# A hybrid decoder block on one core: six SwiGLU pairs from seven products, and the weight sums moved to pay for them

## The chip, the cores and the metric

The kernel runs on one core of a Trainium2 chip. The metric is the device time of one execution, in microseconds; several executions are timed and their median is given. One more execution is recorded by the hardware profiler, and every duration below comes from that one.

## The reference

The block takes 512 rows of 1024 channels in float32. Two token mixers (a Conformer convolution and an RG-LRU) run side by side and are merged through sigmoid gates and a projection. What the change touches is the channel mixer that follows:

```
h = rmsnorm(x, norm2_g)
x = x + (silu(h @ ffn_w1) * (h @ ffn_w3)) @ ffn_w2      # ffn_w1, ffn_w3: 1024 x 2816; ffn_w2: 2816 x 1024
return rmsnorm(x, norm_f_g)
```

## The kernel before

**Products in three parts.** TensorE multiplies float32r. To keep float32's precision every operand is split into a high part (a cast, on ScalarE) and a low part (a subtraction, on VectorE or GpSimd, L113), and a product is the sum of three: high by high, high by low, low by high. A weight chunk is 128 x 1024 values, 512 KB. It is loaded by SyncE's queue into one of four raw buffers (`raws`), cast and split into one of five `hl` buffers, and used by TensorE in 24 matmuls. `weights(key)` sends out the loads of that chunk and of the next four, in a fixed order of chunks.

**Stages, in order.** The input projections (z) follow a list written out by hand, `ORDER`, with 64 steps; the convolution, the gates and the recurrence run beside them on VectorE and ScalarE. GpSimd makes the low parts of the z weights. Then come the two ways out, `yb` (eight steps, weights `lo`) and `ya` (eight steps, weights `co`), then the mixing product `mx`, then the SwiGLU pairs, then the last product `or`, with `ffn_w2`.

**SwiGLU pairs.** The 22 column blocks of the hidden layer are worked in 11 pairs (k and k + 11). A pair of the plain kind takes four chunks, 96 matmuls of 512 columns. Pairs 2 to 5, listed in `SEVEN`, are made by a Strassen-Winograd form: seven block products for eight. Each product takes one chunk, 24 matmuls of 256 columns (`fr`, L1020). Three of the seven weight chunks are quarters of the weights themselves (b11, b21, b22); four are sums of quarters (t1 to t4), read from DRAM. They are used in the order b11, b21, b22, t2, t1, t3, t4. The activations' sums are made by `f_inputs` just before pair 1.

**Who makes the sums.** Those of the SwiGLU weights are made by GpSimd, in `make_f_sums`, a generator that is stepped once per entry of `ORDER` and per step of yb. Every third step it loads a piece (half a chunk's worth of four quarters) into one of three `wsums` buffers; two steps later GpSimd does four operations on it; five weight chunks later SyncE stores it to DRAM. The last product is of seven products too, for all its eleven pairs of blocks, and the sums of its weights (`ows`, then `ot` in DRAM) are made by VectorE, in `make_sums`: two loads of 512 KB into two of the four raw buffers, four operations, four stores of 256 KB. `out_sums` calls it after SwiGLU pairs: two each after pairs 1, 6, 7, 8 and 9, one each after 3 and 5.

**Operands of the last product.** When a pair is complete, `Sevenfold.pair` makes from it five tiles that stay until the last product; those tiles, the activations and their sums share 63 slots (`long`).

**Order on the engines.** Apart from a few stretches written out by hand, a planner orders each engine's instructions: it walks the program in priority of its order and takes what is ready by its own estimate of time. On the chip each queue is then in order. A load that has to wait for its buffer holds up every load behind it on SyncE's queue.

Of the kernel before, what the change touches and what calls it, by code (L numbers as in the profile page):

```python
# [8 lines left out]
F32 = mybir.dt.float32  # L9
F32R = mybir.dt.float32r  # L10
# [3 lines left out]
P = 128  # L14
T = 512
# [25 lines left out]

SEVEN = (2, 3, 4, 5)
SUMS_AT, SUMS_STEP, SUMS_LAG, STORE_LAG = 4, 3, 2, 5


ROWS = [
# [32 lines left out]
def tile_block(ctx, tc, a, out):  # L81
    nc = tc.nc
# [1 line left out]
    consts = pool("consts", 1)  # L84
    raws = pool("raws", RAW)
    hls = pool("hls", HL)
    wsums = pool("wsums", 3)
    psum = pool("psum", 6, space=bass.MemoryType.PSUM)
    psum2 = pool("psum2", 2, space=bass.MemoryType.PSUM)

# [131 lines left out]

    dram = ctx.enter_context(tc.tile_pool(name="dram", bufs=1, space=bass.MemoryType.DRAM))

    class Quartered:
        def __init__(self, name, w, kh, lo, parts=()):

            self.name, self.w, self.kh = name, w, kh
            self.parts = {n: [None] * kh for n in parts}
            self.sums = {(n, k): dram.tile([P, T], F32, tag=f"{name}{n}_{k}", name=f"{name}{n}_{k}") for n in ("t1", "t2", "t3", "t4") if n not in parts for k in range(kh)}  # L230
            self.at = {}

            def quarter(n, k):
                if n[0] == "t":
                    return self.sums[n, k][:, :]
                i, h = int(n[1]) - 1, int(n[2]) - 1
                return w[:, k + kh * i, h * T : (h + 1) * T]

            def chunk(key, of):
                def load(raw_t):  # L240
                    for i, q in enumerate(of):
                        nc.sync.dma_start(raw_t[:, i * T : (i + 1) * T], quarter(*q))

                for i, q in enumerate(of):
                    self.at[q] = (f"{name}{key}", i)
                wchunk(f"{name}{key}", load, len(of), T, lo=lo)


            for p_ in (("b11", "t1", "b21"), ("t2", "t3", "b22"), ("t4",)):
                p_ = [n for n in p_ if n not in parts]  # L250
                for k in range(kh):
                    if len(p_) % 2 and k % 2 == 0:
                        chunk(f"{p_[-1]}_{k}", [(p_[-1], i) for i in (k, k + 1) if i < kh])
                    if len(p_) > 1:
                        chunk(f"{p_[0]}_{k}", [(n, k) for n in p_[:2]])
# [20 lines left out]
        def make_sums(self, k):  # L276
            q = [raws.tile([P, 1024], F32, tag="raw", name=f"{self.name}ws{k}_{i}") for i in range(2)]
            for i, v in enumerate(q):
                nc.sync.dma_start(v, self.w[:, k + self.kh * i, :])
            (q11, q12), (q21, q22) = ((v[:, :T], v[:, T:]) for v in q)  # L280
            sub(vec, q22, q22, q12)
            sub(vec, q12, q12, q11)
            vec.tensor_tensor(out=q11, in0=q22, in1=q11, op=ALU.add)
            sub(vec, q21, q21, q11)
            for n, v in (("t1", q12), ("t2", q11), ("t3", q22), ("t4", q21)):
                if n in self.parts:
                    self.parts[n][k] = split(f"{self.name}{n}{k}", v, vec)
                else:
                    nc.sync.dma_start(self.sums[n, k][:, :], v)

    mixq = Quartered("mx", a["w_mix_out"][0].rearrange("(k p) n -> p k n", p=P), ND // 2, vec, ("t1", "t4"))
    w1 = a["ffn_w1"][0].rearrange("(k p) n -> p k n", p=P)
# [1 line left out]


    KF = NF // 2
    F_SUMS = ("t2", "t1", "t4", "t3")
    f_sums = {k: dram.tile([P, 4, 1024], F32, tag=f"fs{k}", name=f"fs{k}") for k in SEVEN}

    def f_quarter(n, k, w_, c0, c1):  # L300
# [4 lines left out]
    def f_chunk(n, k):  # L305
        def load(raw_t):
            if n[0] == "t":
                nc.sync.dma_start(raw_t, f_sums[k][:, F_SUMS.index(n), :])
            else:
                for i, w_ in enumerate((w1, w3)):  # L310
                    nc.sync.dma_start(raw_t[:, i * T : (i + 1) * T].rearrange("p (k n) -> p k n", k=4), f_quarter(n, k, w_, 0, 4))

        wchunk(f"f{n}_{k}", load, 8, P, lo=vec)

    def make_f_sums():

        todo = [(k, i, c) for k in SEVEN for i in range(2) for c in (0, 2)]
        sums_due, stores_due = [], []  # L320
        n = 0
        while todo or sums_due or stores_due:
            if stores_due and emitted[0] >= stores_due[0][0]:
                stores_due.pop(0)[1]()
            if sums_due and n >= sums_due[0][0]:
                sums_due.pop(0)[1]()
            if todo and n >= SUMS_AT and (n - SUMS_AT) % SUMS_STEP == 0:
                k, i, c = todo.pop(0)
                raw = wsums.tile([P, 1024], F32, tag="wsum", name=f"fws{k}_{i}_{c}")
                q = [raw[:, 256 * m : 256 * m + 256] for m in range(4)]  # L330
                four = (w1, w3)[i].rearrange("p (h k) (e n) -> p h k e n", h=2, e=2)
                with tc.issue_after(newest["load"]):
                    for h in range(2):
                        nc.sync.dma_start(
                            raw[:, h * T : h * T + T].rearrange("p (e k n) -> p e k n", e=2, k=2),
                            four[:, h, c : c + 2, :, k * P : (k + 1) * P].rearrange("p k e n -> p e k n"),
                        )

                def sums(raw=raw, q=q, k=k, at=T * i + P * c):
                    q11, q12, q21, q22 = q  # L340
                    with tc.issue_after(newest["sub"]):
                        sub(pool_e, q22, q22, q12)
                        sub(pool_e, q12, q12, q11)
                        pool_e.tensor_tensor(out=q11, in0=q22, in1=q11, op=ALU.add)
                        sub(pool_e, q21, q21, q11)

                    def stores():
                        with tc.issue_after(newest["load"]):
                            nc.sync.dma_start(f_sums[k][:, :, at : at + 256], raw.rearrange("p (m n) -> p m n", m=4))

                    stores_due.append((emitted[0] + STORE_LAG, stores))

                sums_due.append((n + SUMS_LAG, sums))
            n += 1
            yield
# [437 lines left out]
            mixq.make_sums(j // 2 - 1)  # L793
    yb = sgb
    run_beside(1000)
    for _ in f_sums_steps:
        pass


    add = lambda o, x, y: vec.tensor_tensor(out=o, in0=x, in1=y, op=ALU.add)  # L800
# [8 lines left out]

    class Sevenfold:  # L810
        def __init__(self, q):
            self.q, self.uv, self.ops = q, [], []
            self.name, self.kh = q.name, q.kh

        def tile(self, j, make):

            k, i = j % self.kh, j // self.kh
            if i == 0:
                self.uv.append((longt(f"{self.name}u{k}"), longt(f"{self.name}v{k}")))
            for dst, cs in zip(self.uv[k], HALVES):  # L820
                make(cs, dst[:, HALVES[i]])
            if i:
                self.pair(k, *self.uv[k])

        def pair(self, k, ua, va):

            n = self.name
            u_ = split(f"{n}us{k}", ua, vec)
            s1 = shortt(f"{n}s1{k}")[:, LO]
            add(s1, va[:, LO], va[:, HI])  # L830
            sp = longt(f"{n}s1p{k}", F32R)
            split_to(sp[:, LO], sp[:, HI], s1, vec)
            e = longt(f"{n}e{k}")
            sub(vec, e[:, HI], ua[:, LO], va[:, LO])
            sub(vec, va[:, LO], s1, ua[:, LO])
            sub(vec, e[:, LO], ua[:, HI], va[:, LO])
            self.ops.append((u_, sp, e, va))
# [58 lines left out]
    for n, j in enumerate(mixq.order()):  # L896
        ws = w_tiles(f"co{j}", ND)
        ps = bank(f"ya{j}")
        mm3(ps, ws, un)
        o = sga[j]  # L900
        vec.scalar_tensor_tensor(out=o, in0=ps, scalar=pc("conv_b_out", j), in1=o, op0=ALU.add, op1=ALU.mult)
        m7.tile(j, lambda cs, dst: add(dst, o[:, cs], yb[j][:, cs]))
        if n == 0:
            mixq.make_sums(3)


    x2 = [[longt(f"x2{t}{h}") for h in range(2)] for t in range(NT)]
# [46 lines left out]


    o7 = Sevenfold(outq)
    sums_of = iter(range(KF))

    def out_sums(n):

# [50 lines left out]
    def ffn_seven(k):  # L1011
# [30 lines left out]
        c12 = shortt(f"c12_{k}")  # L1042
        add(c12, r3, q)
        out_of(c12, u_[:, HI])
        product(r7, "s3", "t3")
        c21 = shortt(f"c21_{k}")
        act.copy(c21, r7)
# [3 lines left out]
        add(c21, r1, c21)  # L1051
        out_of(c21, v_[:, LO])
        o7.uv.append((u_, v_))
        o7.pair(k, u_, v_)

    for k in range(1, KF):
        if k in SEVEN:
            ffn_seven(k)
            out_sums(k % 2)
            continue  # L1060
        for j in (k, k + KF):
            p1, p3 = bank(f"f1_{j}"), bank(f"f3_{j}")
            mm3(p1, w_tiles(f"f1_{j}", ND), h2)
            mm3(p3, w_tiles(f"f3_{j}", ND), h2)
            ffn_out(j, p1, p3)
        out_sums(2 if k < KF - 1 else KF)


    x2 = [[longt(f"x2b{t}{h}") for h in range(2)] for t in range(NT)]
# [93 lines left out]
```

## Time and profile before

| | |
|---|---|
| median of 3 runs | 814.86 us (813.67 to 815.19) |
| profiled execution | 814.89 us, of which its span is 813.0 us |
| granted TensorE clock, mean | 0.995 |
| TensorE matmuls busy | 800.0 us, 98% of the span |
| VectorE busy | 644.1 us, 79% |
| ScalarE busy | 443.1 us, 55% |
| GpSimd busy | 210.3 us, 26% |
| DMA | 153.46 MB, 189 GB/s on average |

The span is the time from the first to the last instruction; the execution's own time also holds what lies around it. Busy times overlap between engines. Matmuls are pipelined, so that the durations of single ones overlap too, and a row of the chain, with its length over its count, tells the rate. All times inside the execution are counted from the start of the span.

### The profile page before, as it was taken

To read this page: it belongs to the slowest core of one execution; us is meant where nothing else is said; L and a number is where in the kernel's file an instruction comes from. 1 tells how busy PE (TensorE), PEld (TensorE's weight loads), DVE (VectorE), ACT (ScalarE), POOL (GpSimd) and SP (SyncE) were. 2 spreads that over 40 slices of the span, in tenths; PEclk is the share of its full clock that TensorE was granted. 3 is DMA by queue.
4 is the path that set the end of the run, shared out by engine and by line. 5 is a ranking of instruction groups with operands and counts; after the bars stand their busy time and mean duration, and the time that the engine had idled before them with its cause. 6 is when DMAs were issued, how large, how long until landed. Compare 5 with 4: busy or idle time off the path is not lost.

```text
span 813.0 us, 11453 instructions
## 1 busy us (share of the span) xinstructions
PE 800.0 (98%) x4038; PEld 683.3 (84%) x4038; DVE 644.1 (79%) x1010; ACT 443.1 (55%) x626; POOL 210.3 (26%) x156
## 2 busy tenths in 40 slices
PE   8999999999999999999999999999999999999996
PEld 7988888888887888888888898999988888888884
DVE  4699899998999987777878769797875664688456
ACT  7546688776687755653336554364632223476442
POOL 3565768766675740000000042000000000000000
PEclk9999999999999999999999999999999999999998
DMA  6646475666654522358638535788778778576542
GB/s 209 193 123 171 136 202 176 189 193 198 186 170 130 182 75 65 116 171 263 217 104 259 156 97 176 238 262 248 224 247 282 249 271 297 177 250 216 169 160 104
DMA packets 182029, 153.46 MB, mean 189 GB/s; under 512 B 12519, under 2 KB 150163, under 8 KB 181971
## 3 DMA queue, kind: packets, MB, share of 16 engines
q1 hardware_dynamic: 181971, 152.72, 60.7%
q8 instruction: 32, 0.52, 0.3%
q14 instruction: 26, 0.21, 0.1%
HBM read 123.46 MB, written 26.21 MB: 184 GB/s over the span
## 4 chain that ended last, share of the span: by engine, by line
PE 93%; DVE 4%; issue 1%; DMA 1%; SPq 0%; POOL 0%; ACT 0%; POOLq 0%
PE z L441 31%; PE f L441 19%; PE or L844 13%; PE fr L1020 10%; PE yb L441 7%; PE ya L441 5%; PE mxr L844 5%; DVE cv L600 2%; PE g L721 2%; DMA raw_in<-in_w_in_dram 1%; PE th L481 0%; DVE xb L745 0%; PE tx L481 0%; DVE of L1086 0%; SPq L397 0%
## 5 line engine op out<-in xcount | busy, mean ns | idle before, releaser
L600 DVE SCALAR_TENSOR_TENSOR cv<-u,par,cv 128x511 f32<-128x511 f32 (+17 forms) x240 | 162.6, 729 | 1.1 <-ACT cv L597 0.9
L113 POOL TENSOR_TENSOR hl_in<-raw_in,hl_in 128x1024 fp32r<-128x1024 f32 x52 | 125.5, 2418 | 94.0 <-ACT hl_in L117 92.0
L117 ACT CAST hl_in<-raw_in 128x1024 fp32r<-128x1024 f32 x52 | 54.3, 1044 | 5.9 <-PE z L441 3.0
L117 ACT CAST hl_f<-raw_f 128x1024 fp32r<-128x1024 f32 x28 | 29.3, 1050 | 49.1 <-DMA raw_f<-in_ffn_w_dram 36.0
L113 DVE TENSOR_TENSOR hl_ob<-raw_ob,hl_ob 128x1024 fp32r<-128x1024 f32 (+1 forms) x23 | 27.1, 1178 | 26.8 <-ACT hl_ob L117 26.6
L113 DVE TENSOR_TENSOR hl_f<-raw_f,hl_f 128x1024 fp32r<-128x1024 f32 x28 | 36.2, 1304 | 14.3 <-ACT hl_f L117 14.2
L994 POOL TENSOR_TENSOR hf<-h20h,h20l 128x512 f32<-128x512 f32 x1 | 1.3, 1287 | 171.8 <-DVE h20l L485 171.8
L117 ACT CAST hl_ob<-raw_ob 128x1024 fp32r<-128x1024 f32 (+1 forms) x23 | 23.4, 1015 | 40.3 <-PE or L844 17.4
L441 PE MATMUL z<-h10h,hl_in 128*128 128x512 f32 (+1 forms) x112 | 42.4, 380 | 2.7 <-DVE h10l L485 1.5
L441 PE MATMUL z<-h15h,hl_in 128*128 128x512 f32 (+1 forms) x112 | 42.0, 376 | 0.0
L441 PE MATMUL z<-h16h,hl_in 128*128 128x512 f32 (+1 forms) x112 | 42.0, 376 | 0.0
L441 PE MATMUL z<-h17h,hl_in 128*128 128x512 f32 (+1 forms) x112 | 41.9, 376 | 0.0
L441 PE MATMUL z<-h11h,hl_in 128*128 128x512 f32 (+1 forms) x112 | 41.8, 375 | 0.0
L441 PE MATMUL z<-h12h,hl_in 128*128 128x512 f32 (+1 forms) x112 | 41.8, 375 | 0.0
L441 PE MATMUL z<-h14h,hl_in 128*128 128x512 f32 (+1 forms) x112 | 41.8, 375 | 0.0
L441 PE MATMUL z<-h13h,hl_in 128*128 128x512 f32 (+1 forms) x112 | 41.8, 375 | 0.0
L113 POOL TENSOR_TENSOR fws<-fws 128x256 f32<-128x256 f32 x48 | 36.3, 756 | 2.3
L113 DVE TENSOR_TENSOR ows<-ows,ows 128x512 f32<-128x512 f32 x22 | 15.2, 689 | 20.6 <-DMA ows<-in_ffn_w_dram 20.4
L113 DVE TENSOR_TENSOR hl_ot<-raw_ot,hl_ot 128x1024 fp32r<-128x1024 f32 (+1 forms) x17 | 20.1, 1191 | 11.1 <-ACT hl_ot L117 10.7
L441 PEld LDWEIGHTS z<-h10h,hl_in 128*128 128x128 f32 x112 | 21.3, 191 | 7.4 <-DVE h10l L485 1.8
L117 ACT CAST hl_ot<-raw_ot 128x1024 fp32r<-128x1024 f32 (+1 forms) x17 | 17.5, 1028 | 16.5 <-PE or L844 14.8
L441 PEld LDWEIGHTS z<-h15h,hl_in 128*128 128x128 f32 x112 | 21.4, 191 | 3.8
(905 smaller groups left out, 2574.9 us busy)
## 6 DMA issues: line engine op xcount, KB each, us to landing
raw_in<-in_w_in_dram SPq DMA_DIRECT2D x52, 512.0 KB
raw_f<-in_ffn_w_dram SPq DMA_DIRECT2D x28, 512.0 KB
ows<-in_ffn_w_dram SPq DMA_DIRECT2D x22, 512.0 KB
ot<-ows SPq DMA_DIRECT2D x44, 256.0 KB
raw_ob<-in_ffn_w_dram SPq DMA_DIRECT2D x33, 256.0 KB
raw_ot<-ot SPq DMA_DIRECT2D x33, 256.0 KB
fws<-in_ffn_w_dram SPq DMA_DIRECT2D x32, 256.0 KB
fs<-fws SPq DMA_DIRECT2D x16, 512.0 KB
```

What stands on the lines that cost most here:

```text
L113: return eng.tensor_tensor(out=o, in0=x, in1=y, op=ALU.subtract)
L117: copy(h, full)
L441: pe.matmul(ps, l, r, start=i == 0, stop=i == n - 1)
L600: vec.scalar_tensor_tensor(out=acc[c][:, s:], in0=u[c][:, : T - s], scalar=dw(c, s), in1=acc[c][:, s:], op0=ALU.mult, op1=ALU.add)
L721: pe.matmul(ps, l, r, start=k == 0, stop=k == len(mms) - 1)
L844: pe.matmul(banks[i], l_[:, ts], r_, start=start and n == 0, stop=stop and n == 2, skip_group_check=again)
L994: pool_e.tensor_tensor(out=v, in0=h2p[c][0].bitcast(F32), in1=h2p[c][1].bitcast(F32), op=ALU.add)
L1020: pe.matmul(ps[:, HALVES[i]], lw[:, 4 * i + c, :], rx_, start=not (again or i or c or m), stop=bool(i and c == 3 and m == 2), skip_group_c ...
```

## The change

`SEVEN` grows from four pairs to six, 2 to 7, so GpSimd has 24 pieces to make for 16. It also makes the sums of the first two of the last product's weights (`OUT_EARLY`), four more pieces of the same size, so 28 in all. From step 55 on a piece is begun every second step, and the generator is stepped through the eight steps of ya as well. The other nine sums of the last weights stay with VectorE; `OUT_SUMS` places them after pairs 1 (three), 2, 4, 6, 7 (one each) and 8 (two). A sum is stored by two transfers of 512 KB, since the four sums of a block now lie side by side in DRAM. A pair's operands for the last product are no longer always made at once: those of seven-product pairs wait and are released inside the next pair (pair 6's not before pair 8). For pairs 0 to 2 one of the operands lies in the three `wsums` buffers.

```diff
-SEVEN = (2, 3, 4, 5)
+PIECES = 3
+OUT_EARLY = 2
+OUT_SUMS = {1: 3, 2: 1, 4: 1, 6: 1, 7: 1, 8: 2}
+SEVEN = (2, 3, 4, 5, 6, 7)
 SUMS_AT, SUMS_STEP, SUMS_LAG, STORE_LAG = 4, 3, 2, 5
+SUMS_DENSE = 55
...
+            if not self.parts:
+                for i, v in enumerate(q):
+                    nc.sync.dma_start(self.all_sums[k][:, 2 * i : 2 * i + 2, :], v.rearrange("p (m n) -> p m n", m=2))
+                return
...
-        todo = [(k, i, c) for k in SEVEN for i in range(2) for c in (0, 2)]
+        todo = [f_piece(k, i, c) for k in SEVEN for i in range(2) for c in (0, 2)]
+        todo += [o_piece(k, c) for k in range(OUT_EARLY) for c in range(2)]
...
-            if todo and n >= SUMS_AT and (n - SUMS_AT) % SUMS_STEP == 0:
+            if todo and n >= next_at:
+                next_at += SUMS_STEP - (n >= SUMS_DENSE)
...
             if i:
-                self.pair(k, *self.uv[k])
+                self.waiting.append((k, *self.uv[k]))
+                self.release()
+
+        def release(self, keep=0):
+
+            while len(self.waiting) > keep:
+                self.pair(*self.waiting.pop(0))
...
-            u_ = split(f"{n}us{k}", ua, vec)
+            p_ = None
+            if n == "o" and k < PIECES:
+                both = wsums.tile([P, 1024], F32R, tag="wsum", name=f"{n}us{k}")
+                p_ = both[:, :T], both[:, T:]
+            u_ = split(f"{n}us{k}", ua, vec, p_)
...
         if n == 0:
             mixq.make_sums(3)
+        next(f_sums_steps, None)
+
+    for _ in f_sums_steps:
+        pass
...
-    sums_of = iter(range(KF))
+    sums_of = iter(range(OUT_EARLY, KF))
...
         out_of(c12, u_[:, HI])
+
+        o7.release(max(0, k - 6))
...
-        o7.pair(k, u_, v_)
+        o7.waiting.append((k, u_, v_))
 
     for k in range(1, KF):
         if k in SEVEN:
             ffn_seven(k)
-            out_sums(k % 2)
+            out_sums(OUT_SUMS.get(k, 0))
             continue
+        o7.release()
...
-        out_sums(2 if k < KF - 1 else KF)
+        out_sums(OUT_SUMS.get(k, 0))
```

More of the change, by code (lines that the diff above doesn't have):

```diff
@@ L86, in tile_block @@
     hls = pool("hls", HL)
-    wsums = pool("wsums", 3)
+    wsums = pool("wsums", PIECES)
     psum = pool("psum", 6, space=bass.MemoryType.PSUM)
@@ L223, in tile_block @@
     dram = ctx.enter_context(tc.tile_pool(name="dram", bufs=1, space=bass.MemoryType.DRAM))
+    IN_PLACE = ("t2", "t1", "t4", "t3")
     class Quartered:
@@ L229, in __init__ @@
             self.parts = {n: [None] * kh for n in parts}
-            self.sums = {(n, k): dram.tile([P, T], F32, tag=f"{name}{n}_{k}", name=f"{name}{n}_{k}") for n in ("t1", "t2", "t3", "t4") if n not in parts for k in range(kh)}
+            self.all_sums = [dram.tile([P, 4, T], F32, tag=f"{name}t_{k}", name=f"{name}t_{k}") for k in range(kh)]
+            self.sums = {(n, k): self.all_sums[k][:, i, :] for i, n in enumerate(IN_PLACE) if n not in parts for k in range(kh)}
             self.at = {}
@@ L234, in quarter @@
                 if n[0] == "t":
-                    return self.sums[n, k][:, :]
+                    return self.sums[n, k]
                 i, h = int(n[1]) - 1, int(n[2]) - 1
@@ L288, in make_sums @@
                 else:
-                    nc.sync.dma_start(self.sums[n, k][:, :], v)
+                    nc.sync.dma_start(self.sums[n, k], v)
     mixq = Quartered("mx", a["w_mix_out"][0].rearrange("(k p) n -> p k n", p=P), ND // 2, vec, ("t1", "t4"))
@@ L296, in tile_block @@
     KF = NF // 2
-    F_SUMS = ("t2", "t1", "t4", "t3")
     f_sums = {k: dram.tile([P, 4, 1024], F32, tag=f"fs{k}", name=f"fs{k}") for k in SEVEN}
@@ L307, in load @@
             if n[0] == "t":
-                nc.sync.dma_start(raw_t, f_sums[k][:, F_SUMS.index(n), :])
+                nc.sync.dma_start(raw_t, f_sums[k][:, IN_PLACE.index(n), :])
             else:
@@ L315, in make_f_sums, with f_piece, o_piece @@
     def make_f_sums():
-        todo = [(k, i, c) for k in SEVEN for i in range(2) for c in (0, 2)]
+        def f_piece(k, i, c):
+            four = (w1, w3)[i].rearrange("p (h k) (e n) -> p h k e n", h=2, e=2)
+            at = T * i + P * c
+            halves = [four[:, h, c : c + 2, :, k * P : (k + 1) * P].rearrange("p k e n -> p e k n") for h in range(2)]
+            return f"{k}_{i}_{c}", halves, f_sums[k][:, :, at : at + 256]
+        def o_piece(k, c):
+            four = outq.w.rearrange("p (h k) (e n) -> p h k e n", h=2, e=2)
+            cs = slice(256 * c, 256 * c + 256)
+            return f"o{k}_{c}", [four[:, h, k, :, cs] for h in range(2)], outq.all_sums[k][:, :, cs]
+        todo = [f_piece(k, i, c) for k in SEVEN for i in range(2) for c in (0, 2)]
+        todo += [o_piece(k, c) for k in range(OUT_EARLY) for c in range(2)]
         sums_due, stores_due = [], []
-        n = 0
+        n, next_at = 0, SUMS_AT
         while todo or sums_due or stores_due:
-            if stores_due and emitted[0] >= stores_due[0][0]:
+            if stores_due and (emitted[0] >= stores_due[0][0] or not (todo or sums_due)):
                 stores_due.pop(0)[1]()
@@ L326, in make_f_sums, with sums @@
                 sums_due.pop(0)[1]()
-            if todo and n >= SUMS_AT and (n - SUMS_AT) % SUMS_STEP == 0:
-                k, i, c = todo.pop(0)
-                raw = wsums.tile([P, 1024], F32, tag="wsum", name=f"fws{k}_{i}_{c}")
+            if todo and n >= next_at:
+                next_at += SUMS_STEP - (n >= SUMS_DENSE)
+                name, halves, dest = todo.pop(0)
+                raw = wsums.tile([P, 1024], F32, tag="wsum", name=f"fws{name}")
                 q = [raw[:, 256 * m : 256 * m + 256] for m in range(4)]
-                four = (w1, w3)[i].rearrange("p (h k) (e n) -> p h k e n", h=2, e=2)
                 with tc.issue_after(newest["load"]):
[L333 to L339, printed above, removed]
+                    for h, src in enumerate(halves):
+                        to = raw[:, h * T : h * T + T]
+                        to = to.rearrange("p (e k n) -> p e k n", e=2, k=2) if len(src.shape) == 4 else to.rearrange("p (e n) -> p e n", e=2)
+                        nc.sync.dma_start(to, src)
+                def sums(raw=raw, q=q, dest=dest):
                     q11, q12, q21, q22 = q
@@ L348, in stores @@
                         with tc.issue_after(newest["load"]):
-                            nc.sync.dma_start(f_sums[k][:, :, at : at + 256], raw.rearrange("p (m n) -> p m n", m=4))
+                            nc.sync.dma_start(dest, raw.rearrange("p (m n) -> p m n", m=4))
                     stores_due.append((emitted[0] + STORE_LAG, stores))
@@ L795, in tile_block @@
     run_beside(1000)
-    for _ in f_sums_steps:
-        pass
     add = lambda o, x, y: vec.tensor_tensor(out=o, in0=x, in1=y, op=ALU.add)
@@ L811, in __init__ @@
         def __init__(self, q):
-            self.q, self.uv, self.ops = q, [], []
+            self.q, self.uv, self.ops, self.waiting = q, [], [], []
             self.name, self.kh = q.name, q.kh
@@ L1065, in tile_block @@
             ffn_out(j, p1, p3)
-        out_sums(2 if k < KF - 1 else KF)
+        out_sums(OUT_SUMS.get(k, 0))
+    assert next(sums_of, None) is None
     x2 = [[longt(f"x2b{t}{h}") for h in range(2)] for t in range(NT)]
```

## The prediction

> **What bounds the kernel now.** I read the page first, its busy times and the chain that ended last.
>
> ```profile
> PE 800.0 (98%) x4038; PEld 683.3 (84%) x4038; DVE 644.1 (79%) x1010; ACT 443.1 (55%) x626; POOL 210.3 (26%) x156
> PE 93%; DVE 4%; issue 1%; DMA 1%; SPq 0%; POOL 0%; ACT 0%; POOLq 0%
> ```
>
> TensorE carries 93% of the chain, so an edit pays when it shortens TensorE's own stream and starves it nowhere. The second view is the chain in order of time: start, length, owner, count.
>
> ```profile
> 510.94 80.63 PE fr L1020 x672
> 591.57 108.83 PE f L441 x480
> ```
>
> The first row is pairs 2 to 5 from seven products, the second pairs 6 to 10 from eight (up to 700.40). Both are unbroken, and the list of waits has one TensorE wait behind 463 us, of 0.3 us. The third view is the engines by stage: length; PE, PEld, DVE, ACT and POOL busy, each with its count; clock, DMA share, GB/s.
>
> ```profile
> 489.00:511.00 22.00, 22.00 (x101) 18.27 (x100) 21.57 (x39) 9.63 (x15) 3.37 (x2) 1.00 0.56 188
> 531.00:551.00 20.00, 20.00 (x169) 20.00 (x169) 17.51 (x27) 13.01 (x20) 0.00 (x0) 1.00 0.83 249
> 657.00:679.00 22.00, 22.00 (x99) 18.23 (x98) 13.06 (x23) 6.40 (x9) 0.00 (x0) 1.00 0.85 280
> ```
>
> In pair 1 (first row) VectorE is 98% busy; in a seven-product pair 88%; in an eight-product pair with two weight sums the DMA moves 280 GB/s. The fourth view is SyncE's queue beside pairs 1 and 2, where the sums are loaded (ows) and stored (ot).
>
> ```profile
> 489.81 0.34 SPq L308 DMA_DIRECT2D raw_ft<-fs  x1
> 493.48 5.12 SPq L279 DMA_DIRECT2D ows<-in_ffn_w_dram  x2
> 502.48 0.33 SPq L289 DMA_DIRECT2D ot<-ows  x1
> 503.61 0.33 SPq L279 DMA_DIRECT2D ows<-in_ffn_w_dram  x1
> 504.81 3.47 SPq L289 DMA_DIRECT2D ot<-ows  x3
> 508.48 0.33 SPq L279 DMA_DIRECT2D ows<-in_ffn_w_dram  x1
> 509.10 1.31 SPq L308 DMA_DIRECT2D raw_ft<-fs  x2
> 513.34 6.04 SPq L289 DMA_DIRECT2D ot<-ows  x4
> 520.39 0.32 SPq L308 DMA_DIRECT2D raw_ft<-fs  x1
> ```
>
> The two loads at 509.10 are t1 and t3 of pair 2, its fifth and sixth weights; the one at 520.39 is t4. The last view is VectorE there.
>
> ```profile
> 491.14 2.31 DVE L113 TENSOR_TENSOR hl_fb<-raw_fb,hl_fb 128x1024 fp32r<-128x1024 f32 x1
> 497.03 1.22 DVE L113 TENSOR_TENSOR hl_fb<-raw_fb,hl_fb 128x1024 fp32r<-128x1024 f32 x1
> 518.35 0.68 DVE L113 TENSOR_TENSOR ows<-ows,ows 128x512 f32<-128x512 f32 x1
> 519.29 2.35 DVE L113 TENSOR_TENSOR hl_ft<-raw_ft,hl_ft 128x1024 fp32r<-128x1024 f32 x2
> ```
>
> **Part 1, two more pairs from seven products.** By the chain's first row a 256-column product takes 80.63/672 = 0.1200 us; a pair has 7 x 24 = 168 of them, 20.16 us. By the second a 512-column one takes 108.83/480 = 0.2267 us; a pair has 96, 21.77 us. Each pair saves 1.61 us, not an eighth, because half the columns take 53% of the time (PEld is busy throughout the 531:551 row). Two pairs give -3.22 us, all on the path.
>
> Beside that, each gains three weight splits on ScalarE and VectorE (3 x 1.05 and 3 x 1.22 us) and its drains. The 531:551 row already has such a pair with a sum in it, at 17.51 of 20 us on VectorE: hidden. Weights are 7 x 0.524 = 3.67 MB in 20.16 us, 182 GB/s; with one sum (2.1 MB) 286, about the 280 of the 657:679 row. Pairs 6 and 7 each have one: cost 0, at most 1 us. The held-back operands of a pair (release) are wanted only from 700 us on; VectorE is 59% busy in the 657:679 row, so they cost 0 as well. Three of them use the slots that GpSimd's pieces leave free, a relief if anything.
>
> **Part 2, twelve more pieces on GpSimd.** A piece is four subtractions at 0.756 us (the page's fws group), 3.0 us; twelve are 36 us. In 260:314 GpSimd is busy 27.8 of 54 us and idle in 314:463, so its own time costs 0. Each piece also puts two loads (0.65 us) and a store (0.60) on SyncE's queue, 23 us in all, ahead of the weight loads of lo and co, and 1 MB of traffic into stages at 119 to 201 GB/s. Three buffers serve them, a piece every two steps, and a buffer is held for two steps plus five weight chunks: about seven steps where six are to be had. So SyncE will wait for the store of an earlier piece; in the profile it does so six times, at most 5.3 us. Behind that wait stands the next lo weight; the tightest is ready (split) at 354.68 and wanted at 359.16, slack 4.5 us. I take 0; the other end is a wait of 5 us.
>
> VectorE pays too: its split of 128x1024 took 2.31 us beside a GpSimd addition and 1.22 without (first two rows of the last fence). Four or five pieces, 12 to 15 us, fall beside the yb stage (325:380), where VectorE has 13.6 us free of 55. [...]
>
> **Part 3, the sums of the last weights.** Two move to GpSimd; each of the other nine still costs VectorE four operations of 0.69 us, and stores become two of 512 KB for four of 256. Pairs 9 and 10 are freed, where nothing waited: 0. The new thing is three sums after pair 1 for two, and then seven-product pairs with a weight due every 2.88 us instead of 5.44. Program order puts the third sum's two loads ahead of t1 of pair 2. All four raw buffers would then hold sums 2 and 3, and t1 waits until sum 2 is stored.
>
> What that costs: t1 is wanted at 510.94 + 4 x 2.88 = 522.46. Now its split ends at 519.29 + 1.22 = 520.5, slack 2.0. Sum 2's last operation ends at 519.03 and a store frees its buffer about 2.1 us after issue (506.42 to 508.48), so t1 would be loaded near 520.3 instead of 509.10. The load at 520.39 was followed by its cast at 524.85; with cast 1.05 and split 1.22, t1 would be ready at 527.1: late by 4.6 us. The t3, t4 and pair-3 weights then follow in time. Ends: 0, if t1 and t3 keep the buffers of 509.1, and 6 us, if VectorE delays sum 2 by the third's 2.8 us. I take 0, narrowly: the trace does not show which transfer is planned first, it shows t1 and t3 going ahead of the second sum's four stores, and TensorE lost nothing there although VectorE was full.
>
> **The sum.** The profiled execution took 814.89 us (span 813.0 and 1.9 around it), against a median of 814.86. 814.89 - 3.22 = 811.7 us.
>
> **The rivals.** *Stall at pair 2 (slower or level).* As worked out: 811.7 + 4.6 = 816.3; between 815.2 and 817.7 for a stall of 3.5 to 6. It speaks for it that SyncE's loads follow program order all along the fence, against it that the order is planned anew. It decides when the stall passes 3.2 us. A short one, 1.6 to 3.5 us, when only the second load of sum 3 comes first, gives 813.3 to 815.2.
>
> *Stall with a slower clock.* At the start TensorE stood from 10.0 to 11.5 us, after transposes, and the stretches 11.2:14.6 and 14.6:20 have a granted clock of 0.78 and 0.83, so 3.4 x 0.22 + 5.4 x 0.17 = 1.7 us were lost, as by 3.3 us at half clock. The same behind a 4.6 us gap costs 1.7 us: 816.3 + 1.7 = 818.0. [...]
>
> *Pieces starve yb.* A SyncE wait of 5 us, or VectorE filled by contention, spends the 4.5 us of slack and a further 3 to 6 us: 814.7 to 817.7.
>
> *No gain from the pairs.* That the added pairs run slower than pairs 2 to 5 has nothing for it; they are the same code.
>
> **How the numbers follow.** What a measurement of this kernel can tell from no change is 0.2%, 1.6 us: faster is below 813.2, slower above 816.5. Clean 0.44, faster. Short stall 0.10, same. Long stall 0.22: 0.08 same, 0.14 slower. Stall and clock 0.12, slower. Starved yb 0.12, half same, half slower. Together 0.44 faster, 0.24 same, 0.32 slower. Clean has its own range, 811.2 to 812.7 (0.5 us below for the spread of the runs, the 1 us of Part 1 above); the full one runs from 811.2 to 818.0, which leaves out half of the clock case and little else.
>
> **What would show it.** Right: six pairs in 121 us, 1008 products at 0.120 us, no TensorE wait behind 463 us, and t1 of pair 2 loaded ahead of the third sum. Wrong: a gap in TensorE four products into pair 2, ended by ScalarE's or VectorE's hl_ft, with raw_ft on SyncE behind six ows loads; a granted clock below 1.00 after it; or a gap in yb ended by hl_lo, with SyncE waiting on fs.

## The result and the profile after

| kernel | median us | lowest to highest | runs | ratio to before in the same call |
|---|---|---|---|---|
| before | 813.67 | 813.39 to 815.19 | 5 | |
| changed | 821.90 | 821.63 to 822.76 | 5 | 1.0098 [1.0084, 1.0113] |

The change costs 1%, 8.2 us. The forecast was 811.7, and 821.9 lies above the range. The profiled execution took 821.9 us; its span is 820.1 against 813.0, so 7.1 us are to be found in the traces. The page's busy times and chain first:

```profile
PE 801.3 (98%) x4182; PEld 690.0 (84%) x4182; DVE 659.6 (80%) x1018; ACT 454.1 (55%) x642; POOL 254.8 (31%) x204
PE 86%; DVE 8%; DMA 2%; issue 1%; SPq 1%; ACT 1%; POOL 1%; POOLq 0%; DVEq 0%
```

TensorE's share of the chain falls from 93% to 86%: it now waits somewhere. The chain in order of time shows where (start, length, owner, count; shorter rows between these are left out):

```profile
517.29 3.52 DMA ot<-ows
520.83 4.50 DMA raw_ft<-fs
526.43 1.24 DVE hl_ft L120
527.71 4.78 PE fr L1060 x22
533.84 1.23 DVE hl_ft L120
535.11 107.82 PE fr L1060 x884
642.94 65.31 PE f L468 x288
```

Before's row of seven-product pairs, unbroken from 510.94, is broken here in pair 2. The chain runs through a store of a sum, then a load of t1, its split, 22 products, then a second split. Behind 535.11 the chain stays on TensorE. Pairs 2 to 7 last from about 510.8 to 642.94, 132.1 us, where 1008 products at 0.1200 us are 121.0. The list of waits names the same two tiles (total us, times, longest):

```profile
PE fr L1060 <- ACT hl_ft L124: 4.5, 2, 4.1
PE fr L1060 <- DVE hl_ft L120: 2.0, 2, 1.5
```

SyncE's queue beside pairs 1 and 2 answers why t1 is late:

```profile
493.36 10.45 SPq L290 DMA_DIRECT2D ows<-in_ffn_w_dram  x3
506.29 1.86 SPq L298 DMA_DIRECT2D ot<-ows  x2
508.96 2.17 SPq L290 DMA_DIRECT2D ows<-in_ffn_w_dram  x3
517.29 1.79 SPq L298 DMA_DIRECT2D ot<-ows  x2
520.83 0.32 SPq L322 DMA_DIRECT2D raw_ft<-fs  x1
521.31 1.04 SPq L298 DMA_DIRECT2D ot<-ows  x2
522.40 5.31 SPq L322 DMA_DIRECT2D raw_ft<-fs  x2
```

Six ows loads stand ahead of t1. Sums 2 and 3 hold all four raw buffers from 511 us on, and t1 goes out at 520.83, 3.5 us after sum 2's first store was issued. Before, it went out at 509.10. Last, the engines by stage across the two gaps (length; PE, PEld, DVE, ACT, POOL busy with counts; clock, DMA share, GB/s):

```profile
522.00:525.10 3.10, 0.33 (x3) 0.12 (x2) 0.01 (x1) 0.58 (x1) 0.00 (x0) 1.00 0.84 274
525.10:528.50 3.40, 1.59 (x5) 1.30 (x6) 1.23 (x1) 1.04 (x1) 0.00 (x0) 0.51 1.01 353
528.50:531.90 3.40, 3.40 (x17) 3.40 (x17) 0.00 (x0) 1.05 (x1) 0.00 (x0) 0.50 0.95 265
531.90:535.40 3.50, 1.59 (x11) 1.19 (x10) 2.86 (x4) 2.40 (x3) 0.00 (x0) 0.99 0.77 200
535.40:538.80 3.40, 3.40 (x18) 3.40 (x18) 3.40 (x5) 1.58 (x2) 0.00 (x0) 0.50 0.73 201
```

Three stretches of 3.4 us have half the clock (0.51, 0.50, 0.50). From one product's start to the next, TensorE's gaps are 522.05 to 526.45 and 526.83 to 527.71 (t1), 532.43 to 533.09 and 533.32 to 535.11 (t3). The first of t3's two ends with the cast of t4, two of whose products are queued there, the second with t3's own split. Less the 0.12 us of a product for each, t1 cost 5.0 us and t3 2.2. The 23 steps from product to product between 527.71 and 532.43 took 4.72 us where 2.76 is their time at full clock, and the 120 products of 535 to 551 took 15.9 where 14.4 is: 3.5 us for the clock. Together 10.7 us lost against 3.4 us gained (measured below) is close to the 7.1 of the spans.

### The profile page after: what moved, and what is told of

The parts are those of the page before. It is cut to its first block, busy times and chain, and to the rows that moved or that the text cites. A ratio compares the mean times of both kernels' runs of the same rounds, so it can differ in the third digit from the quotient of the medians.

```text
span 820.1 us, 11842 instructions
## 1 busy us (share of the span) xinstructions
PE 801.3 (98%) x4182; PEld 690.0 (84%) x4182; DVE 659.6 (80%) x1018; ACT 454.1 (55%) x642; POOL 254.8 (31%) x204
## 4 chain that ended last, share of the span: by engine, by line
PE 86%; DVE 8%; DMA 2%; issue 1%; SPq 1%; ACT 1%; POOL 1%; POOLq 0%; DVEq 0%
PE z L468 29%; PE fr L1060 14%; PE or L880 13%; PE f L468 11%; PE yb L468 7%; PE ya L468 5%; PE mxr L880 5%; DVE cv L627 2%; PE g L748 2%; DMA raw_in<-in_w_in_dram 1%; SPq L424 1%; DVE hl_fb L120 1%; DMA raw_ft<-fs 1%; DVE hl_ft L120 0%; PE th L508 0%
## 5 line engine op out<-in xcount | busy, mean ns | idle before, releaser
L120 POOL TENSOR_TENSOR fws<-fws 128x256 f32<-128x256 f32 x72 | 60.2, 838 | 31.5 <-DMA fws<-in_ffn_w_dram 28.3
L1060 PE MATMUL fr<-hs_0h,hl_ft 128*128 128x256 f32 x192 | 37.9, 294 | 4.6 <-ACT hl_ft L124 4.1
L120 DVE TENSOR_TENSOR hl_ft<-raw_ft,hl_ft 128x1024 fp32r<-128x1024 f32 x24 | 29.2, 1220 | 14.0 <-ACT hl_ft L124 14.0
L120 DVE TENSOR_TENSOR hl_f<-raw_f,hl_f 128x1024 fp32r<-128x1024 f32 x20 | 26.8, 1338 | 14.3 <-ACT hl_f L124 14.2
L124 ACT CAST hl_ft<-raw_ft 128x1024 fp32r<-128x1024 f32 x24 | 25.1, 1049 | 22.7 <-DMA raw_ft<-fs 22.4
L1060 PEld LDWEIGHTS fr<-hs_0h,hl_ft 128*128 128x128 f32 x192 | 32.1, 202 | 5.1 <-ACT hl_ft L124 4.3
L124 ACT CAST hl_f<-raw_f 128x1024 fp32r<-128x1024 f32 x20 | 20.9, 1049 | 24.6 <-DMA raw_f<-in_ffn_w_dram 19.8
L120 DVE TENSOR_TENSOR hl_ot<-raw_ot,hl_ot 128x1024 fp32r<-128x1024 f32 (+1 forms) x17 | 20.1, 1190 | 11.1 <-ACT hl_ot L124 10.7
L120 DVE TENSOR_TENSOR hl_fb<-raw_fb,hl_fb 128x1024 fp32r<-128x1024 f32 x18 | 23.1, 1283 | 6.8 <-ACT hl_fb L124 6.7
```

What stands on the lines that cost most here:

```text
L120: return eng.tensor_tensor(out=o, in0=x, in1=y, op=ALU.subtract)
L124: copy(h, full)
L1060: pe.matmul(ps[:, HALVES[i]], lw[:, 4 * i + c, :], rx_, start=not (again or i or c or m), stop=bool(i and c == 3 and m == 2), skip_group_c ...
```

## The experiments

The theory from here: two weight sums in flight hold all four raw buffers, a third behind pair 1 makes t1 wait for a store, and clock and t3 follow from that. The rivals are that the pairs or GpSimd's pieces are at fault, that VectorE is too full, and that only the order of loads is. Where no range of times is given, a kernel was run once.

**1. The third sum moved behind pair 9, all else kept.**

```diff
-OUT_SUMS = {1: 3, 2: 1, 4: 1, 6: 1, 7: 1, 8: 2}
+OUT_SUMS = {1: 2, 2: 1, 4: 1, 6: 1, 7: 1, 8: 2, 9: 1}
```

> The changed kernel with the third sum moved from behind pair 1 to behind pair 9, nothing else. Buffers theory (the two loads of sum 3 take the raw buffers that t1 and t3 of pair 2 need, so that t1 waits for sum 2 to be stored): t1 is loaded near 509 us again, no gap of TensorE in pair 2, no half clock; the span falls by the 11 us lost there, from 820.1 to 809 (808.5 to 810.5), 3 to 4 us below the kernel before. GpSimd theory (the twelve more pieces and their traffic cost the time): the span stays above 815. Seven-product theory (pairs 6 and 7 run slower than pairs 2 to 5): the span stays above 812, and the six pairs take more than 122 us.

Measured: 810.56 us (810.39 to 811.37, 5 runs), before 814.29 in the same call, ratio 0.9950 [0.9936, 0.9964]. SyncE's queue of this kernel, beside pairs 1 and 2:

```profile
509.17 0.33 SPq L290 DMA_DIRECT2D ows<-in_ffn_w_dram  x1
509.56 1.79 SPq L322 DMA_DIRECT2D raw_ft<-fs  x2
...
```

and its chain:

```profile
511.00 40.74 PE fr L1060 x338
...
551.75 80.66 PE fr L1060 x670
632.41 65.31 PE f L468 x288
```

t1 and t3 leave at 509.56, and 1008 products run from 511.00 to 632.41 without a gap, 0.1204 us each. The span, 809.6, is 3.4 us below before's, near the 3.22 expected of two pairs with nothing lost to the pieces. So one sum's place turns -3.7 us into +8.2. This version beats both kernels.

**2. Before, with nothing changed but a third sum after pair 1** (so that none is left for pair 9).

```diff
-        out_sums(2 if k < KF - 1 else KF)
+        out_sums(3 if k == 1 else 2 if k < KF - 1 else KF)
```

> The kernel before (four pairs from seven products, sums stored in four transfers) with three sums behind pair 1 and one fewer at the end. Buffers theory: the same gap without any other part of the change: t1 of pair 2 is loaded near 521 us for 509, gaps of 5 to 8 us in pair 2 with one or two stretches of half clock; span 821 to 825, against 813. If the loss needs another part of the change (six pairs, the stores of 512 KB, the held-back operands): no gap above 2 us, span 813 to 815.

Measured: 822.79 us, span 820.9, 7.9 above before's. The loss needs neither the pairs, nor the pieces, nor the stores of 512 KB. Its list of waits of TensorE:

```profile
PE fr L1020 <- ACT hl_ft L117: 4.1, 1, 4.1
```

Its chain:

```profile
520.68 4.63 DMA raw_ft<-fs
...
527.69 71.73 PE fr L1020 x574
```

And VectorE there:

```profile
529.83 1.23 DVE L113 TENSOR_TENSOR hl_ft<-raw_ft,hl_ft 128x1024 fp32r<-128x1024 f32 x1 [2.20 <-ACT hl_ft L117]
532.79 0.69 DVE L800 TENSOR_TENSOR q<-fr,q 128x512 f32<-128x512 f32 x1 [1.73 <-PE fr L1020]
```

t1 is loaded at 520.68, as in the changed kernel, and the gap is the same (522.01 to 527.69, with two products in between). But there is no second one: behind 527.69 the row is unbroken. VectorE splits t3 at 529.83, ahead of the addition to q. In the changed kernel it stands behind it:

```profile
526.43 1.23 DVE L120 TENSOR_TENSOR hl_ft<-raw_ft,hl_ft 128x1024 fp32r<-128x1024 f32 x1 [4.42 <-ACT hl_ft L124]
532.51 0.69 DVE L825 TENSOR_TENSOR q<-fr,q 128x512 f32<-128x512 f32 x1 [4.86 <-PE fr L1060]
...
533.84 2.35 DVE L120 TENSOR_TENSOR hl_ft<-raw_ft,hl_ft 128x1024 fp32r<-128x1024 f32 x2
```

VectorE idles 4.86 us for TensorE's t1 product, itself late and at half clock, while t3, cast by 530.83, waits behind. That is the second gap: the order suits a t1 that comes in time.

**3. TensorE kept busy through the wait for t1** by 36 products of 256 columns into a bank that is written anew afterwards.

```diff
         act.copy(q, r1)
+        if k == 2:
+            for _ in range(36):
+                pe.matmul(r7[:, LO], h2p[0][0][:, :P], h2p[0][0][:, LO], start=True, stop=True)
         product(r5, "s1", "t1")
```

> The changed kernel with 36 spare matmuls of 256 columns (4.3 us) ahead of the fifth product of pair 2, in the place where TensorE stands; their result is overwritten. If the two stretches of half clock come from the standing engine: t1 is ready at 527.7 us as before, its product then takes 2.9 us for 4.8, VectorE's sum behind it and the low part of t3 come 2 us earlier, clock 1.00 throughout; span near 816.5. If the clock falls for another reason, or the spare matmuls only shift the work: span 820 or more.

Measured: 819.43 us, span 817.6. The clock is 1.00 from 510 to 643 us, and 2.5 us of the changed kernel's span are gone. I had expected 3.6. Not the clock alone differs: VectorE's order was planned anew with the edit, and t3's split now stands ahead of the addition to q:

```profile
531.27 1.23 DVE L120 TENSOR_TENSOR hl_ft<-raw_ft,hl_ft 128x1024 fp32r<-128x1024 f32 x1 [3.05 <-ACT hl_ft L124]
532.41 0.69 DVE L825 TENSOR_TENSOR q<-fr,q 128x512 f32<-128x512 f32 x1
```

So t3 costs 0.9 us here (at 531.5) for 2.2. Beside the wait that the spare products fill, TensorE stands twice more for 0.9 us: for t1's split (at 527.2), which cost 0.8 in the changed kernel too, and for a split of pair 4's weights (at 558.8). The three make 2.8 us; t1's split and t3 together cost 3.0 in the changed kernel. So the waits are nearly as long, the clock's part is about 3 us, and most of the loss is waiting for data. That the gap at t3 shrinks when its split goes first agrees with experiment 2.

**4. A fifth raw buffer**, paid for by two of the 63 slots.

```diff
-SLOTS, SHORT = 63, 5
-RAW = 4
+SLOTS, SHORT = 61, 5
+RAW = 5
```

> The changed kernel with five raw buffers for four (two of the 63 long slots given up for it); the order of the queue stays, three sums stay behind pair 1. Buffers theory: the first sum starts one buffer earlier (near 490 us for 493.4), t1 is loaded near 509 us, no gap above 1 us in pair 2; span 809 to 811. Load theory: the same VectorE work and the same bytes in the same stretch, so a gap of 3 us or more stays, span above 814.

Measured: 814.86 us (813.67 to 815.90, 10 runs), ratio 1.0003 [0.9994, 1.0013]. SyncE loads t1 at 511.23 with the three sums in place, and the gap in pair 2 shrinks to 1.3 us (522.02 to 523.37), the clock staying at 1.00. That is what buffers as the cause would do. What is left of the gap is VectorE's:

```profile
515.19 1.06 ACT L124 CAST hl_ft<-raw_ft 128x1024 fp32r<-128x1024 f32 x1 [0.18 <-DMA raw_ft<-fs]
...
522.08 2.36 DVE L120 TENSOR_TENSOR hl_ft<-raw_ft,hl_ft 128x1024 fp32r<-128x1024 f32 x2
```

t1 is cast by 516.25, but VectorE, which has no idle time from 509.4 to 522.1, splits it only at 522.08, behind operations on sums and activations. So the rival of the full VectorE is right for about 1.2 us, a share that does not show in the changed kernel, where the load itself came later. And 809 to 811 was missed, as two new gaps of 1.1 and 2.2 us come at 549.0 and 590.4. TensorE's waits:

```profile
PE fr L1060 <- ACT q L1079: 2.7, 2, 1.9
...
```

ScalarE at the first of the two gaps:

```profile
548.52 1.05 ACT L124 CAST hl_fb<-raw_fb 128x1024 fp32r<-128x1024 f32 x1 [4.49 <-DMA raw_fb<-in_ffn_w_dram]
549.47 0.58 ACT L1079 COPY q<-fr 128x512 f32<-128x512 f32 x1
```

The copy that frees a bank of TensorE's stands behind a cast that waited 4.49 us for a load. At the second, larger gap it stands behind a cast (590.98) that waited 4.39 us for TensorE's own products, so no load was late there. Whether the two slots less have a part in that was not separated.

**5. The order alone**: sums 2 and 3 after pair 1 kept, but three steps of weights taken ahead of the third.

```diff
+        if k == 1:
+            out_sums(2)
+            emit_to(emitted[0] + 3)
+            out_sums(1)
+            continue
         out_sums(OUT_SUMS.get(k, 0))
```

> The changed kernel with three sums behind pair 1, but t1, t3 and t4 of pair 2 are requested after the second sum and ahead of the third. The work is the same, the order differs. Buffers theory: t1 and t3 are loaded at 509 to 510 us and there is no gap at the fifth product of pair 2; the third sum then holds two buffers ahead of the first weights of pair 3, so a gap of up to 4 us may appear in pair 3; span 809 to 814. Load theory (VectorE is full and the third sum's 2.8 us of operations and 2 MB of traffic are what makes t1 late): a gap of at least 3 us in pair 2 stays, span above 815.

Measured: 818.70 us, a miss. t1 and t3 leave at 508.52 and there is no gap before t1 in pair 2; instead six gaps of 0.8 to 1.4 us lie between 529.9 and 554.7, and then 3.5 us at half clock. There sum 3 (loads at 520.15, stores from 530.61 on) and then pair 2's own sum (loads at 534.62, stores from 544.55 on) hold two of the four buffers one after the other. The waits:

```profile
PE fr L1060 <- ACT hl_fb L124: 2.1, 2, 1.2
PE fr L1060 <- DVE hl_ft L120: 1.4, 2, 0.8
...
```

Another order moves the shortage behind t1, mostly to pair 3; it doesn't end it.

**6. Two sums after pair 1 and two after pair 2.** Pair 2 to 3 is the place where VectorE is not as full as in pair 1 (88% busy for 98% in the kernel before).

```diff
-OUT_SUMS = {1: 3, 2: 1, 4: 1, 6: 1, 7: 1, 8: 2}
+OUT_SUMS = {1: 2, 2: 2, 4: 1, 6: 1, 7: 1, 8: 2}
```

> The changed kernel with two sums behind pair 1 and two behind pair 2, for three and one. Buffers theory (two sums together hold all four raw buffers, and a seven-product pair asks for a weight every 2.9 us): no gap in pair 2, a gap of 3 to 6 us at the fifth product of pair 3, where t1 waits for a sum to be stored; span 813 to 818. VectorE theory (pair 1 is the place that is full, at 98%; pair 2 has 12% free): no gap above 1 us anywhere, span 809 to 811.

Measured: 823.86 us, span 822.1, above the expected 813 to 818. TensorE's longest wait in the pairs (the next is 0.5 us):

```profile
PE fr L1060 <- ACT hl_ft L124: 10.4, 1, 10.4
```

SyncE's queue beside pairs 2 and 3:

```profile
527.46 0.34 SPq L322 DMA_DIRECT2D raw_ft<-fs  x1
529.36 5.59 SPq L290 DMA_DIRECT2D ows<-in_ffn_w_dram  x4
539.18 5.37 SPq L298 DMA_DIRECT2D ot<-ows  x4
544.60 2.10 SPq L322 DMA_DIRECT2D raw_ft<-fs  x3
```

Pair 2 is clean. In pair 3 four ows loads fill the four buffers, and t1 leaves only at 544.60, behind both sums' stores: a gap from 542.21 to 552.90. VectorE is busy 11.2 of the 20 us from 531 to 551, so it isn't the limit. I had expected a gap of 3 to 6 us; a sum more costs its whole time from load to store here.

**7. Three sums at once where plain pairs follow** (after pair 8).

```diff
-OUT_SUMS = {1: 3, 2: 1, 4: 1, 6: 1, 7: 1, 8: 2}
+OUT_SUMS = {1: 2, 2: 1, 4: 1, 6: 1, 7: 1, 8: 3}
```

> The changed kernel with the third sum of pair 1 moved behind pair 8: two behind 1, three behind 8. If three sums in a row are the harm wherever they stand, a gap of 4 us or more appears in pair 9 or 10, span above 813. By the buffers theory it depends on what comes next: behind pair 8 stand plain pairs, which ask for a weight every 5.4 us, not 2.9, and their four chunks are loaded before the sums; no gap, span 809 to 810.5, as with the sum behind pair 9.

Measured: 811.85 us. The chain has pairs 2 to 7 in one row, and the eight-product pairs behind three sums go on from them unbroken:

```profile
511.92 120.95 PE fr L1060 x1008
632.87 65.31 PE f L468 x288
...
```

Three sums did no harm here, where a chunk is due every 5.44 us, for every 2.88 in a seven-product pair.

**8. Pairs 2 to 8 from seven products**, pieces begun every second step from step 46.

```diff
-OUT_SUMS = {1: 3, 2: 1, 4: 1, 6: 1, 7: 1, 8: 2}
-SEVEN = (2, 3, 4, 5, 6, 7)
+OUT_SUMS = {1: 2, 2: 1, 4: 1, 6: 1, 9: 2, 10: 2}
+SEVEN = (2, 3, 4, 5, 6, 7, 8)
...
-SUMS_DENSE = 55
+SUMS_DENSE = 46
```

> Seven pairs (2 to 8) from seven products, two sums behind pair 1, one behind 2, 4 and 6, two behind 9 and 10; a piece every second step from step 46 on. By the sum that held for six pairs (1.6 us a pair) and no stall: 1.6 us below the kernel with two sums behind pair 1, span 808, near 0.993 of the kernel before. Against it: 32 pieces end in a burst behind ya, and pairs 7 and 8 both follow without a plain pair between; a gap there or in the mixing product would bring it to 811 or more.

Measured: 828.68 us (827.01 to 833.50), ratio 1.0200 [1.0176, 1.0224], a clear miss. The seven pairs are as wanted in its chain:

```profile
518.76 141.11 PE fr L1060 x1176
```

But its waits name the stages on either side of them:

```profile
PE or L880 <- ACT hl_ob L124: 6.2, 2, 5.6
PE mxr L880 <- DVE x L825: 2.9, 2, 1.5
...
```

Seven pairs take 0.1200 us a product, no gap. The pieces now end so late that loads of mx stand behind them on SyncE's queue (the first load of its sums, raw_mxt, goes out at 432.96, behind a store of a piece at 428.00; in the changed kernel at 416.54). And the sums after pairs 9 and 10 hold buffers that the last product wants: SyncE waits 4.1 us for their stores, and TensorE has a gap from 721.4 to 727.3, with 6.8 us at half clock that begin within it.

**9. Seven such pairs, with a sum behind each of them.** All eleven sums stay with VectorE.

```diff
-OUT_EARLY = 2
-OUT_SUMS = {1: 3, 2: 1, 4: 1, 6: 1, 7: 1, 8: 2}
-SEVEN = (2, 3, 4, 5, 6, 7)
+OUT_EARLY = 0
+OUT_SUMS = {1: 2, 2: 1, 3: 1, 4: 1, 5: 1, 6: 1, 7: 1, 8: 1, 9: 2}
+SEVEN = (2, 3, 4, 5, 6, 7, 8)
```

> Seven pairs (2 to 8) from seven products; GpSimd makes their sums alone (28 pieces at the steps of the changed kernel) and none of the last weights; VectorE makes eleven: two behind pairs 1 and 9, one behind each of 2 to 8. Buffers theory: one sum between two seven-product pairs was harmless behind pairs 2, 4, 6 and 7, so one behind each is: no gap, 1176 products in 141 us, span 808 (807.5 to 809), 0.993 of the kernel before. Against it: sums behind every pair ask for 286 GB/s through seven pairs, where the stage of two sums moved 280, and delays add up from pair to pair; then gaps of 1 to 4 us from pair 4 on and a span of 811 or more.

Measured: 824.82 us (822.43 to 826.90), ratio 1.0127 [1.0109, 1.0145], a miss as well. Pairs 2 to 8 take 157.5 us where 141.1 would do. Twelve gaps of 0.4 to 2.2 us from 559.9 on make 11.7 us of it, and behind some of them the clock falls (0.52 from 563.0 to 566.5, 0.79 from 593 to 600; 0.98 over 511 to 669). TensorE's waits:

```profile
PE fr L1060 <- ACT q L1079: 3.9, 3, 1.4
PE fr L1060 <- DVE hl_ft L120: 2.1, 5, 1.0
PE fr L1060 <- ACT c L1072: 2.0, 1, 2.0
```

The longest are those of the five-buffer kernel, ScalarE's copies late behind casts (at 561.51, 594.59 and 664.34 behind casts that had waited 2.3 to 4.8 us for a load). With two sums after pair 1 and one each after 2, 4, 6 and 7 nothing waited; with one behind each pair TensorE does. Whether a seventh pair can pay stays open: both tries failed at other places.

## Why the prediction was wrong

**Part 1, right.** Two more pairs were put at -3.22 us and "hidden" otherwise. From the start of pair 2 to TensorE's end, before takes 292.4 us, the kernel with three sums at pair 8 289.2 and the one with two sums after pair 1 289.7; the rest of the latter's -3.4 in the span, 0.7, lies behind TensorE's end. The chain with three sums at pair 8 has the 121 us and 0.1200 us a product that the prediction asked for.

**Part 2, right in its result, low on its means.** No product of yb, ya or mx waits on account of the pieces, and the starved-yb rival is out. GpSimd grew by 44.5 us for 48 operations, 0.93 us each where I had put 0.756, and SyncE's waits for the store of an earlier piece (L364) from 16.9 us in six to 48.1 in thirteen, 6.4 at most. Both fell on time that TensorE didn't need: 34 of the 48 us of waits lie between 250 and 330 us, ahead of the lo weight that the prediction named as the tightest. That is in part luck, since the prediction put the harmful wait at 5 us and did not work out where the waits would fall. That VectorE loses beside yb what the pieces take there, 12 to 15 us, was the author's estimate, and no run shows it: from 325 to 380 GpSimd was busy 15.8 us, and VectorE 40.8 for 41.4 before. Single operations took longer (a split at 355.33 1.36 us for 0.82), and GpSimd's own took longer too: two at 351.80 4.2 us, where two took 1.5 at 333.02. From 380 to 423 the clock is 1.00 and TensorE full, at a DMA share of 0.88.

**Part 3, the step that failed.** The working found the stall: t1 "would be loaded near 520.3", "ready at 527.1: late by 4.6 us". It was loaded at 520.83 and its split ended at 527.66, and TensorE went on at 527.71. I then wrote "I take 0, narrowly", on the ground that t1 and t3 went ahead of the second sum's four stores. That ground was no evidence: in that trace (509.10 against 513.34) buffers were free for them, and the prediction had just counted that there would be none. The third sum alone, put into the kernel before, costs 7.9 us with t1 loaded at 520.68.

**What followed it was undersized.** "The t3, t4 and pair-3 weights then follow in time" was wrong in the changed kernel: t3 was loaded 1.6 us after t1 and cast only at 529.78, with t1, two stores and t4 beside it and 353 GB/s from 525.1 to 528.5. Its split was then queued behind the addition to q: 2.2 us. The slow clock was put at 1.7 us from the start-up, and took 3.5, as three stretches of 3.4 us were hit and not one and a part. So 818.0, the forecast of the rival with the clock, lacked 2.2 for t3, 1.8 of the clock and 0.4 of the first gap; with the 0.2 by which part 1 gained more, this makes 822.2 against the 821.9 measured.

How long TensorE has to stand for the clock to fall is not shown. TensorE was busy 0.33 us of the 3.10 from 522.00 on, before the first of the three slow stretches, 1.59 of the 3.40 before the second and 1.59 of the 3.50 before the third: it stood for a part of each, and for all of none.

**Chances.** Clean had 0.44 and stall with clock 0.12. The range ended at the clock rival with the 4.6 us stall in it; with the 6 us end that Part 3 itself gave, it would have reached 819.4, still short by the t3 gap.

## What to carry to other kernels

Count the buffers that everything planned ahead of a load will hold, and from when until when: if they are all held, the load waits for the store that frees one (here t1's went out at 520.83 us for 509.10), and another order only moves the shortage (in experiment 5 to six gaps of 0.8 to 1.4 us). A working that ends in a dated stall shouldn't be overruled by a trace in which a buffer was free. When one operand comes late, look in each engine's order for what was planned behind its consumer (here t3's split, 2.2 us), and add that and the clock (here 3.5 us) to the stall.

## What the runs showed of the hardware

- In the changed kernel three stretches of 3.4 us, from 525.1, 528.5 and 535.4 us on, had a granted clock of 0.51, 0.50 and 0.50. Its gap of 4.4 us had 6.8 us at half clock and one of 10.7 us (two sums after pair 2) about 10 us, both beginning within the gap; but stretches with TensorE partly busy (1.59 of 3.50 us in the changed kernel; 1.77 of 3.00 where the third sum goes behind three steps of weights) had 3.4 and 3.5 us at half clock behind them too (0.50, 0.51), whereas a single gap of 2.2 us with five buffers had none (1.00 from 592.6 to 600).
- In the changed kernel the same 512 KB load of a sum took 4.5 us to its cast when issued at 520.83, and 7.4 us when issued at 522.40 with other transfers beside it (353 GB/s from 525.1 to 528.5).
